# A fifth staging buffer for the rows of weights, and five list tiles a half for the batched heads, in a one-core decoder block

## The chip, the core and the metric

The kernel runs on one core of a Trainium2 chip. The metric is the device time of one execution in microseconds (us); three runs of the kernel before are at hand, and their median is what a changed kernel is compared with. The engines are named as in the profile: PE is the matrix engine and PEld its weight loads, DVE the vector engine, ACT the scalar engine, POOL the engine that issues the gathers, SP the one that issues most plain transfers.

## The reference

The kernel computes one decoder block over 1024 tokens of width 1024 in float32: a first part with gated linear attention and a spatial gate beside it, and then an expert mixer, whose lists of experts are what half of the change is about. Cut to what matters:

```
proj = h @ w_in                       # 1024 x 7184, then attention, gates, w_out
q  = (h2 @ w_q).reshape(T, 8 heads, 2, 128)
s1 = q[..., 0, :] @ keys1.T ; s2 = q[..., 1, :] @ keys2.T
v1, i1 = top_k(s1, 16) ; v2, i2 = top_k(s2, 16)
top_s, pos = top_k(v1[:, None] + v2[None, :], 16)    # per token and head
g = softmax(top_s)                                   # 16 weights
y = sum over heads and the 16 experts: g * gelu(expert_down[e] . h2) * expert_up[e]
```

With the scales of the inputs the softmax is steep: most of the 16 weights of a head are zero in float32. The kernel counts weights of at least 1.18e-38. Worked out from the reference's inputs, 65 heads of the first half of the tokens and 51 of the second still have an eighth weight that large; the kernel calls them rare. All their weights that large are 634 rows in the first half and 475 in the second.

## The kernel before

The tokens are worked off in two halves of 512. Each half streams its weights in rows of 128x512 float32 (256 KB): 14 groups of 8 for the projection, 32 for the output projection, 40 for the queries, so 184 for a half. Such a row goes through three stages. SP fetches it into one of `WT` staging buffers `wt` (line 1373, pool `wstage`, line 1055). ACT makes its rounded part `wh` (L1377) and DVE the rest `wl` (L1379), into one of `WS` = 4 pairs of buffers; a staging buffer is free again when `wl` has been made. PE then multiplies: 12 matrix products of 512 columns for a row, 6 in the output projection (L182, L183, L185, or L188 to L190 for the first and last rows of a group). `weights_ahead` keeps four rows (LOOK + 1) issued ahead of the one that is used.

The expert mixer works on list tiles of 128 experts. POOL gathers 1 MB for a tile (128 rows of `tab` with 8 KB each, `uv`, L526), or 512 KB twice (`uvu`, `uvv`) where the tile goes into two 4 KB buffers; PE brings the tokens' rows to the entries (`hps`, L579 and L580), DVE makes the dot products (L581), ACT the Gelu (L584), and PE adds the weighted rows up (L626 and L627 while the first part is still running, L607 afterwards). There are three kinds of tiles. Ordinary lists: 9 tiles (`NT`) for each block of 128 tokens. Direct tiles, the best expert of each head, one for each head of a block (`Wd`, L535 to L540; those of the first four blocks are made by `direct_rows`, L753 to L776, which only POOL, DVE and ACT work on). And the lists of the rare heads, batched for a half: `NTR` tiles, which read the table `thq`/`tlq` with 50 columns. Their room is `t * 128` rows for `t` tiles; `peer_rest` compares it with the counts and works everything off again in a slow loop if any list does not fit.

`peer_stream` writes the order of all tiles in one list `todo`: the rare tiles of the first half first, then the lists of blocks 0 to 3, then 12 direct tiles of later blocks, after which it waits until the first part is over (`HOLD`). This is called stage 1 here; in it `wh` and `wl`, attention and list tiles share the engines. The rest, from the gather of the 19th direct tile on, is stage 2. Which buffers a tile gets follows from its place k in `todo`: `RING[k % 6]` in stage 1, `RING9[k % 9]` in stage 2, where 0 is the pool of stage 1 (three buffers), 1 the 4 KB buffers and 2 the pool that opens with stage 2.

The program is recorded by Tile with a list scheduler, which orders the instructions of every engine by times that it expects, so a number at the top of the file can move instructions everywhere. Each engine then works in its written order, and so do POOL's gathers.

```
NTR = (6, 6)
WS = 4
WT = 4
RING = (1, 0, 1, 0, 2, 0)
RING9 = (2, 0, 1, 2, 0, 2, 1, 0, 2)
        seg(NBLK, range(PH, PH + NTR[0]))
        seg(NBLK + 1, range(PH, PH + NTR[1]))
        caps = [NT * P] * NBLK + [t * P for t in NTR] + [P] * NG
        wst_p = pa.enter_context(tc.tile_pool(name="wstage", bufs=WT))
```

Of the kernel before, what the change touches and what calls it, by code (L numbers as in the profile page):

```python
# [40 lines left out]
ROW0 = (0, 16, 24, 32, 40, 44, 48, 52, 56)  # L41
NC_ = 64
NT = 9
NTR = (6, 6)
EB = 2
WS = 4
WT = 4
RD = 0.62
UVC = 4
RING = (1, 0, 1, 0, 2, 0)  # L50
# [31 lines left out]
def block_kernel(ctx: ExitStack, tc: tile.TileContext, x, xT, cT, w_ada, b_ada, b_adaT, n1T, w_inp, w_alr,  # L82
# [697 lines left out]
    def peer_stream():  # L780
# [3 lines left out]
        def seg(b, js, open_=True, close=True):  # L784
            if open_:
                opens.add((b, js[0]))
            if js[0] < PH:
                runs.add((b, js[0]))
            todo.extend((b, j) for j in js)
            if close:  # L790
                closes.add((b, js[-1]))

        rows = range(PH, last + 1)
        seg(NBLK, range(PH, PH + NTR[0]))
        for b in range(BH):
# [8 lines left out]
        seg(BH + 1, range(PH, last))  # L804
        seg(NBLK + 1, range(PH, PH + NTR[1]))
        seg(BH + 2, range(PH, last - 1), close=False)
# [138 lines left out]
    def peer_rest(pl, pg_):  # L945
# [5 lines left out]
        morei = pc.tile([1, 1], I32, name="morei")  # L951
        caps = [NT * P] * NBLK + [t * P for t in NTR] + [P] * NG
        for i, c in enumerate(caps):
# [100 lines left out]
    with ExitStack() as pa:  # L1054
        wst_p = pa.enter_context(tc.tile_pool(name="wstage", bufs=WT))
        wsp = pa.enter_context(tc.tile_pool(name="wsplit", bufs=WS))
# [831 lines left out]
```

## Time and profile before

| what | value |
| --- | --- |
| three runs | 1444.07, 1448.06, 1449.47 us; median 1448.06 |
| the profiled execution | 1445.78 us, of which the profile's span is 1444.0 |
| instructions | 19662 |
| mean granted PE clock | 0.974 of full speed |
| matrix products of a row of weights, one line's group (L182) | 648, 397 ns each as recorded |
| gathers of 1 MB for list tiles | 73, 8.2 us from issue to landing in the median |

The profile's page lists busy time by engine, the chain of work that ended last, and the groups of equal instructions. Matrix products overlap, and a recorded duration is longer than the distance from one start to the next; that distance is read from the chain of waits or the timeline. A row of the timeline is: start, duration, engine, line, operation, tile written <- tiles read, count, and in brackets how long the engine had been idle before it and what ended that. A row of the waits is: who waited <- for whom: us in total, times, the longest.

### The profile page before, as it was taken

Reading aid. Unit: us, or ns where it says so; the run is one execution under the profiler, and the core shown is the slowest. Engines: PE = TensorE matmul, PEld = TensorE weight load, DVE = VectorE, ACT = ScalarE, POOL = GpSimd, SP = SyncE. Lnnn points to the kernel's source line nnn. Section 1 sums busy time; section 2 is a strip of 40 time slices with the busy share of each in tenths; the row PEclk is TensorE's granted clock in tenths of the full one; section 3 lists DMA queues with packets and bytes.
Section 4 is the critical chain, followed back from the end, with each engine's and each line's share of the span. In section 5 each row is a group of like instructions: output and inputs, shape, how many; then the busy total and the mean of one; then the engine's idle time right before and its main releaser. Section 6 shows DMA issues by size and latency. Waiting matters only on the chain.

```text
span 1444.0 us, 19662 instructions
## 1 busy us (share of the span) xinstructions
PE 1352.7 (94%) x6018; PEld 1041.6 (72%) x6018; DVE 1094.8 (76%) x3109; ACT 728.8 (50%) x1602; POOL 287.2 (20%) x276
## 2 busy tenths in 40 slices
PE   8999999999998999979989999899987999789996
PEld 6678777888887888767877878787766886445553
DVE  7885686433578589888889787778788877899775
ACT  4463333332455456456435677456545555546542
POOL 0100011000000111341542143211021114553331
PEclk9999999999999999999999999999999999999999
DMA  9743553322377675675777698886777658998984
GB/s 332 274 166 117 190 163 129 95 95 66 114 243 255 216 244 184 242 250 199 246 265 262 223 347 308 305 287 229 254 277 275 228 194 350 330 372 329 418 308 173
DMA packets 120980, 345.00 MB, mean 239 GB/s; under 512 B 15049, under 2 KB 24521, under 8 KB 108962
## 3 DMA queue, kind: packets, MB, share of 16 engines
q0 software_dynamic: 32208, 165.95, 31.5%
q1 hardware_dynamic: 71600, 133.43, 27.7%
q10 hardware_dynamic: 17058, 44.29, 8.5%
q8 instruction: 48, 0.79, 0.2%
q14 instruction: 66, 0.54, 0.1%
HBM read 319.40 MB, written 24.23 MB: 238 GB/s over the span
## 4 chain that ended last, share of the span: by engine, by line
PE 37%; DVE 9%; DMA 9%; issue 7%; ACT 4%; POOL 2%; SPq 0%; ACTq 0%; DVEq 0%; POOLq 0%
PE acc L607 6%; PE mm L182 5%; PE mm L183 5%; PE mm L185 5%; PE mm L188 2%; PE mm L189 2%; PE mm L190 2%; DMA uv<-in_tab_dram,ix 2%; PE aux L1781 2%; DMA uv<-in_tab_dram,dix 1%; DMA uvd<-in_down_dram,dix 1%; PE hps L579 1%; PE hps L580 1%; DVE uv L581 1%; DVE wl L1379 1%
## 5 line engine op out<-in xcount | busy, mean ns | idle before, releaser
L1377 ACT ACTIVATE wh<-wt 128x512 fp32r<-128x512 f32 x360 | 223.0, 628 | 333.8 <-PE mm L183 113.6
L1379 DVE TENSOR_TENSOR wl<-wt,wh 128x512 fp32r<-128x512 f32 x360 | 242.2, 683 | 140.9 <-ACT wh L1377 78.6
L182 PE MATMUL mm<-wh,hTh 128*128 128x512 f32 x648 | 256.9, 397 | 5.6 <-ACT wh L1377 5.6
L183 PE MATMUL mm<-wh,hTl 128*128 128x512 f32 x648 | 254.8, 394 | 0.0
L185 PE MATMUL mm<-wl,hTh 128*128 128x512 f32 x648 | 200.2, 396 | 0.0
L182 PEld LDWEIGHTS mm<-wh,hTh 128*128 128x128 f32 x648 | 122.3, 189 | 35.7 <-ACT wh L1377 7.7
L183 PEld LDWEIGHTS mm<-wh,hTl 128*128 128x128 f32 x648 | 122.1, 189 | 25.8 <-issue 0.7
L185 PEld LDWEIGHTS mm<-wl,hTh 128*128 128x128 f32 x648 | 121.1, 188 | 26.8 <-issue 0.7
L526 POOL DMA_INDIRECT uv<-in_tab_dram,ix x73 | 81.9, 1122 | 268.0 <-ACT ix L558 163.0
L182 PE MATMUL mm<-hTh,wh 128*128 128x512 f32 x240 | 96.5, 402 | 0.0
L183 PE MATMUL mm<-hTl,wh 128*128 128x512 f32 x240 | 96.2, 401 | 0.0
L188 PE MATMUL mm<-wh,hTh 128*128 128x512 f32 x216 | 86.8, 411 | 2.7 <-DVE sg L1605 1.0
L581 DVE SCALAR_TENSOR_TENSOR uv<-uv,hps 128x512 f32<-128x512 f32 x110 | 73.7, 680 | 17.4 <-PE hps L580 8.7
L189 PE MATMUL mm<-wl,hTh 128*128 128x512 f32 x216 | 85.5, 397 | 0.0
L190 PE MATMUL mm<-wh,hTl 128*128 128x512 f32 x216 | 85.4, 395 | 0.0
L188 PE MATMUL mm<-hTh,wh 128*128 128x256 f32 (+1 forms) x208 | 72.1, 350 | 12.6 <-DVE q L1509 7.8
L189 PE MATMUL mm<-hTl,wh 128*128 128x256 f32 (+1 forms) x208 | 70.4, 340 | 3.3 <-DVE hTl L174 3.3
L753 POOL DMA_INDIRECT uvd<-in_down_dram,dix x32 | 36.9, 1154 | 174.2 <-DVE cidx L354 38.2
L185 PE MATMUL mm<-hTh,wl 128*128 128x512 f32 x240 | 71.0, 397 | 0.0
L190 PE MATMUL mm<-hTh,wl 128*128 128x256 f32 (+1 forms) x208 | 69.1, 339 | 0.3 <-DVE wl L1379 0.3
L619 DVE SCALAR_TENSOR_TENSOR vl<-uv,r,vh 128x512 fp32r<-128x512 f32 x82 | 59.9, 745 | 11.9 <-ACT vh L618 5.7
L579 PE MATMUL hps<-hh,E 128*128 128x512 f32 x132 | 61.3, 465 | 6.1 <-DVE uv L581 2.8
(971 smaller groups left out, 2936.4 us busy)
## 6 DMA issues: line engine op xcount, KB each, us to landing
wt<-in_w_inp_dram SPq DMA_DIRECT2D x224, 256.0 KB, 3.5
wt<-in_w_qp_dram SPq DMA_DIRECT2D x80, 256.0 KB, 4.9
wada<-in_w_ada_dram SPq DMA_DIRECT2D x32, 512.0 KB, 5.3
wt<-in_w_outp_dram SPq DMA_DIRECT2D x64, 256.0 KB, 3.8
wada<-in_w_ada_dram SPq DMA_DIRECT2D x32, 256.0 KB, 5.7
s_d<-so ACTq DMA_DIRECT2D x28, 256.0 KB, 2.6
xr<-in_x_dram ACTq DMA_DIRECT2D x8, 512.0 KB, 4.6
x_d<-x ACTq DMA_DIRECT2D x8, 512.0 KB, 4.2
```

The source lines that it names most:

```text
L182: nc.tensor.matmul(ps, lh, rh, start=False, stop=False)
L183: nc.tensor.matmul(ps, *((lh, rl) if feat else (ll, rh)), start=False, stop=False)
L185: nc.tensor.matmul(ps, *((ll, rh) if feat else (lh, rl)), start=False, stop=False)
L188: nc.tensor.matmul(ps, lh, rh, start=first, stop=False)
L189: nc.tensor.matmul(ps, lh, rl, start=False, stop=False)
L190: return nc.tensor.matmul(ps, ll, rh, start=False, stop=last).ins
L526: nc.gpsimd.indirect_dma_start(out=dst[:], out_offset=None, in_=src, in_offset=off)
L579: nc.tensor.matmul(hps, Ej, hh[:, sl], start=True, stop=False)
L581: nc.vector.scalar_tensor_tensor(uv[0][:, sl], uv[0][:, sl], 1.0, hps, op0=OP.mult, op1=OP.mult, accum_out=r[:, 2 + n:3 + n])
L607: ins = nc.tensor.matmul(acc[:, sl], W, v[:, sl], start=first, stop=last).ins
L1377: nc.scalar.activation(wh, wt, AF.Identity)
L1379: nc.vector.tensor_tensor(wl, wt, wh.bitcast(F32), op=OP.subtract)
```

## The change

Two numbers at the top of the file:

```
-NTR = (6, 6)
+NTR = (5, 5)
 EB = 2
 WS = 4
-WT = 4
+WT = 5
```

`WT = 5` adds a staging buffer of 2 KB in each partition. `NTR = (5, 5)` takes the sixth list tile of the rare heads out of each half: 2 of 1 MB gathers (the two 512 KB gathers of a tile count as one), and on PE 2 times 2 products of L549/L550, 8 of L579/L580 in all, 4 of L626/L627 in the first half and 4 of L607 in the second, with their dots and Gelus on DVE and ACT. The room for rare rows is then 640 in each half. Every later tile moves up one place in `todo` (two places behind the second half's rare tiles), and so takes another turn of `RING` or `RING9`.

On SP, at the start of the weights of the first half (L1089 is the hand-ordered first group, `wada` are rows of the modulation's weights):

```order
 L1089 DMA wada<-in_w_ada_dram 128x2x256 x8
-L1089 DMA wt<-in_w_inp_dram 128x512
-L1108 DMA wada<-in_w_ada_dram 128x1024
-L1089 DMA wt<-in_w_inp_dram 128x512
+L1089 DMA wt<-in_w_inp_dram 128x512 x2
 L1089 DMA wal<-in_w_al_dram 16x512
 L1089 DMA balt<-in_b_alT_dram 128x4
 L1089 DMA keyst<-in_keysT_dram 128x256
 L1089 DMA sgub<-in_sgu_bT_dram 128x8
-L1373 DMA wt<-in_w_inp_dram 128x512 x4
+L1108 DMA wada<-in_w_ada_dram 128x1024
+L1373 DMA wt<-in_w_inp_dram 128x512 x5
```

Five rows of weights now go out in one go where four did, and a `wada` row that stood between two of them moved behind the first group.

On ACT, in the second half while `direct_rows` runs (`rdr` is a direct tile's Gelu, `dt`, `eGi`, `egl` the exponentials that the attention's products wait for, `wh` the rounded weights):

```order
-L770 ACTIVATE yd<-uvd,rdr 128x1024
 L1567 ACTIVATE egl_5818<-G_5482 128x4x2
 L1522 ACTIVATE eGi<-G_5458 128x512
-L1523 ACTIVATE dt<-dt 128x512 x2
+L1523 ACTIVATE dt<-dt 128x512
+L767 ACT_TABLE_LOAD
+L767 ACTIVATE rdr<-rdr 128x1
+L1523 ACT_TABLE_LOAD
+L1523 ACTIVATE dt<-dt 128x512
 L1377 ACTIVATE wh<-wt 128x512 x3
 L767 ACT_TABLE_LOAD
```

A Gelu now stands between the two `dt`, with a load of the function table on each side of it, and ahead of three conversions of weights.

On POOL, where stage 2 begins, the first gather into the new pool is the row that waits for many transfers (DMAHW) and engines at once. Before:

```order
L526 DMA uvv<-in_up_dram,dix_2_137 128x1024 [waits DMASW3_49,DVE_49]
L526 DMA uv<-in_tab_dram,dix_2_137 128x2048 [waits DMAHW2_49,DMAHW3_49,DMAHW1_49,DMAHW5_49,DMAHW0_49,DMAHW6_49,DMASW4_49,DMAHW7_49,PE_49,Activation_49]
L526 DMA uv<-in_tab_dram,dix_2_137 128x2048 [waits DMASW5_49,PE_49]
L526 DMA uv<-in_tab_dram,dix_2_137 128x2048 [waits DMASW7_49,DMASW6_49,PE_49]
L526 DMA uv<-in_tab_dram,dix_3_138 128x2048 [waits DVE_49]
```

and of the change:

```order
L526 DMA uvu<-in_down_dram,dix_2_137 128x1024 [waits DMASW0_49,DVE_49]
L526 DMA uv<-in_tab_dram,dix_2_137 128x2048 [waits DMAHW3_49,DMAHW2_49,DMAHW4_49,DMAHW1_49,DMAHW5_49,DMAHW0_49,DMAHW6_49,DMASW1_49,DMAHW7_49,PE_49,Activation_49]
L526 DMA uv<-in_tab_dram,dix_2_137 128x2048 [waits DMASW2_49]
L526 DMA uv<-in_tab_dram,dix_2_137 128x2048 [waits DMASW3_49,PE_49]
L526 DMA uvv<-in_up_dram,dix_2_137 128x1024 [waits DMASW4_49,DVE_49]
```

Before, the gather into the new pool is followed by two that wait for PE to be through with a buffer of the old pool; now the next one waits for no engine, and only the one behind it does.

## The prediction

> **What bounds the kernel now.** First the page: busy time by engine, the chain of work that ended last, and the transfers.
>
> ```profile
> PE 1352.7 (94%) x6018; PEld 1041.6 (72%) x6018; DVE 1094.8 (76%) x3109; ACT 728.8 (50%) x1602; POOL 287.2 (20%) x276
> ...
> PE 37%; DVE 9%; DMA 9%; issue 7%; ACT 4%; POOL 2%; SPq 0%; ACTq 0%; DVEq 0%; POOLq 0%
> ...
> DMA packets 120980, 345.00 MB, mean 239 GB/s; under 512 B 15049, under 2 KB 24521, under 8 KB 108962
> ```
>
> PE is busy for 94% of the span by the record. Its idle time is thus 91 us of 1444. So the kernel is bound by PE, and a change pays in two ways: it takes products away, or it closes one of PE's gaps. Second, stretches by windows (start and end, length, busy us of PE, PEld, DVE, ACT, POOL, the granted PE clock, the DMA engines' busy share, GB/s), where the change touches something:
>
> ```profile
> 300.00:400.00 100.00, 100.00 (x482) 84.00 (x481) 44.07 (x87) 35.69 (x59) 0.00 (x0) 1.00 0.30 97
> ...
> 640.00:650.00 10.00, 2.48 (x11) 1.71 (x10) 8.14 (x24) 3.12 (x7) 3.06 (x3) 0.77 1.03 405
> ...
> 770.00:800.00 30.00, 28.96 (x130) 23.79 (x129) 29.68 (x68) 18.14 (x38) 8.85 (x7) 1.00 0.73 251
> ...
> 1055.00:1060.00 5.00, 2.95 (x13) 2.07 (x12) 3.38 (x8) 0.51 (x1) 1.00 (x1) 1.00 1.04 413
> ...
> 1250.00:1255.00 5.00, 3.71 (x9) 1.80 (x10) 4.39 (x36) 2.66 (x8) 1.15 (x2) 1.00 0.80 306
> 1255.00:1260.00 5.00, 1.71 (x4) 0.40 (x3) 4.84 (x29) 3.49 (x5) 4.08 (x4) 0.98 0.94 318
> ...
> 1320.00:1356.00 36.00, 35.35 (x126) 20.72 (x125) 30.81 (x135) 19.65 (x71) 18.02 (x19) 1.00 0.99 397
> ```
>
> From 300 to 400 us, in the first half of the tokens, where no list tiles run, PE has no gap at all and the transfers are at 0.30; nothing is to be won there. Where the first rare tiles run (770 to 800 us), PE and DVE are both full. Where the second ones run (1320 to 1356), PE is full and the transfers nearly so. In between lie gaps: at 640, at 1055, at 1250, each time with the transfers at 0.8 to 1.04 of what they can do.
>
> **The list tiles.** The chain around 1335 us, in order of time (start, us, what), and the rare tiles' own group:
>
> ```profile
> 1336.86 1.72 PE acc L607 x4
> ...
> 1338.71 0.33 PE hps L579
> 1339.03 0.23 PE hps L580
> ...
> 1339.50 0.23 PE hps L580
> ...
> 1339.73 1.72 PE acc L607 x4
> ...
> L549 PE MATMUL tps<-thq,E x6: 587/587/587, 1332.3 to 1346.6; 128*128 128x50 f32 x6
> ```
>
> The six tiles of the second half's rare heads lie between 1332.3 and 1346.6, on PE and on the chain without a break, one every 2.87 us (1336.86 to 1339.73). One fewer is **-2.9 us**. If the transfers set the pace there instead, 1 MB at 397 GB/s is 2.6 us, so the bounds are -2.6 and -2.9, and I take PE's.
>
> A tile of the first half costs PE 8 products of 512 columns: four `hps`, and four of L626/L627. At 0.23 us from start to start (the L580 above) that is 1.84, and the two narrow products of L549/L550 add about 0.1: **-1.9 us**. DVE loses two dots of 0.68 and two splits of 0.745 (groups below), about 2.9 us with what stands between them, so DVE, full there as well, doesn't hold the gain back. Bounds: 0, if another wait takes its place, and -2.9, DVE's share.
>
> ```profile
> L581 DVE SCALAR_TENSOR_TENSOR uv<-uv,hps 128x512 f32<-128x512 f32 x110 | 73.7, 680 | 17.4 <-PE hps L580 8.7
> ...
> L619 DVE SCALAR_TENSOR_TENSOR vl<-uv,r,vh 128x512 fp32r<-128x512 f32 x82 | 59.9, 745 | 11.9 <-ACT vh L618 5.7
> ```
>
> **The fifth staging buffer.** It lets SP fetch a row of weights when the `wl` five rows back is made, not four. It can pay only where PE waits for a conversion that waits for a transfer. Waits of ACT and PE over the whole program, PE's two rows at 1060 us, and the `wl` that free the buffers there:
>
> ```profile
> ACT wh L1377 <- DMA wt<-in_w_inp_dram: 42.8, 20, 5.2
> ...
> ACT wh L1377 <- DMA wt<-in_w_outp_dram: 23.9, 15, 5.5
> ...
> PE mm L182 <- ACT wh L1377: 5.6, 3, 3.1
> ...
> 1060.17 0.50 PE L182 MATMUL mm<-wh,hTh 128*128 128x512 f32 x1 [2.22 <-ACT wh L1377]
> ...
> 1064.61 0.79 PE L182 MATMUL mm<-wh,hTh 128*128 128x512 f32 x1 [3.09 <-ACT wh L1377]
> ...
> 1052.06 11.79 DMA wt<-in_w_outp_dram
> ...
> 1065.41 0.43 PE mm L183
> ...
> 1050.75 1.28 DVE L1379 TENSOR_TENSOR wl<-wt,wh 128x512 fp32r<-128x512 f32 x2
> ```
>
> ACT waits 67 us for rows of weights in these two groups, but PE only 5.6 us for ACT, and 5.3 of them are the two rows at 1060. So nearly all of ACT's waiting is already hidden behind split rows in stock. The chain there runs through one transfer of 11.79 us, in a stretch where the engines move 413 GB/s. The second stall ends when that row lands. With a fifth buffer it goes out one `wl` earlier, and two `wl` make 1.28 us, so 0.64; and one row less is queued ahead of it, 0.262 MB at 413 GB/s = 0.63. Together -1.3 us; closing the first stall brings PE only sooner to the second. With the third of PE's waits (0.3) that is **-1.6 us**. The bounds: 0, and all of it, 5.6 us, plus the slower pace behind the stall, where seven products stand 0.43 apart and not 0.23, 1.4 us: -7.0. The value near the low end follows the full transfer engines at 1055.
>
> On this the Trainium skill ("DMA: Bandwidth & Descriptors", section "Issuing engines are not separate DMA queues") says that transfers from every issuing engine end up on the same 16 DMA engines and interleave. The 413 GB/s at a share of 1.04 agree: a transfer that starts earlier takes the place of another one there. By this rule the buffer brings nothing in a full stretch, which is rival 1.
>
> **The turn of the buffers at the start of stage 2.** Three rows of POOL and one of PE:
>
> ```profile
> 1243.72 0.94 POOL L526 DMA_INDIRECT uv<-in_tab_dram,dix  x1 [1.55 <-PE aux L1781]
> ...
> 1246.67 0.94 POOL L526 DMA_INDIRECT uv<-in_tab_dram,dix  x1 [2.00 <-PE acc L607]
> ...
> 1253.55 0.94 POOL L526 DMA_INDIRECT uv<-in_tab_dram,dix  x1 [5.94 <-PE acc L607]
> ...
> 1260.90 3.75 PE L607 MATMUL acc<-uv,Wd 128*128 128x512 f32 x4 [4.20 <-issue]
> ```
>
> The first gather into the new pool goes out at 1243.72. The next two wait 2.00 and 5.94 us for PE to release a buffer of the old pool, and POOL's whole queue stands behind them, while PE runs dry for 4.20 us at 1256.7. In the changed order the second gather goes into the new pool too and waits for no engine. What this can win is the transfer time that lay idle: 5 us at 0.80 and 5 us at 0.94 leave 1.3 us. **-1.3 us**; bounds 0 (the transfers are full right behind) and -4.2, PE's whole gap.
>
> **Everything else that moves.** The other moves on the engines I cost at 0 in the middle, since each Gelu and conversion is still there once; the shown place on ACT adds two table loads of 1.28 us to an engine that is half idle. Where that cover is gone is rival 2.
>
> The sum: -2.9 - 1.9 - 1.6 - 1.3 = **-7.7 us**. The profiled execution of 1445.78 us, span and what lies around it, becomes 1438.1. It lies 2.3 us below the median of the three runs, 1448.06, to which the same -7.7 gives **1440.4 us**. A measurement of this kernel can tell about 0.5%, 7.2 us, from no change, so the forecast is barely outside that.
>
> **Rival 1: the fifth row only displaces gathers.** For it: the full stretches at 640 and 1055. In 900 to 1130 us the chain runs through long landings of gathers:
>
> ```profile
> 988.54 7.67 DMA uv<-in_tab_dram,ix
> ...
> 1029.57 8.93 DMA uv<-in_tab_dram,ix
> ...
> 1111.12 7.61 DMA uv<-in_tab_dram,ix
> ```
>
> If each of the three lands one row later (0.63), the change gives back 1.9, staging wins nothing, and the turn of the buffers nothing either: -2.9 - 1.9 + 1.9 = -2.9, 1445.2 us. Against it: over the span the transfers run at 239 GB/s, so most extra rows find room.
>
> **Rival 2, slower: a Gelu ahead of the conversions on ACT.** Its place is 620 to 700 us, where `direct_rows` shares ACT with the attention. A Gelu there waits for DVE's dot, the dot for a gather, and ACT works in order, so everything behind it stands too.
>
> ```profile
> ACT rdr L767 <- DVE uvd L765: 23.7, 10, 6.2
> ...
> PEld mm L188 <- ACT rdr L767: 8.2, 1, 8.2
> ...
> 650.26 0.76 PE L188 MATMUL mm<-hTh,wh 128*128 128x512 f32 x1 [7.78 <-DVE q L1509]
> ...
> 626.72 1.14 ACT L1523 ACTIVATE dt<-dt 128x512 f32<-128x512 f32 x2
> ...
> 627.98 1.22 DVE L765 SCALAR_TENSOR_TENSOR uvd<-uvd,h2d 128x1024 f32<-128x1024 f32 x1
> ```
>
> Before, such waits came to 23.7 us on ACT and reached PE once, for 8.2 us. In the changed order a Gelu stands ahead of a `dt` that was made before 627.9, while the dot it needs began at 627.98: with 1.2 us for the dot and two loads of 1.28 the `dt` and three conversions come nearly 5 us later. It decides when the Gelu's wait outlasts the split rows in stock, four at 12 times 0.23 us, 11 us. One more stall of 8.2 us eats the gain (1448.6), two make it slower: -7.7 + 16.4 = +8.7, 1456.8 us. Against it: in that same gap PE's product was released by DVE, so ACT was not last even there, and one place in ACT's order need not make two stalls.
>
> **Rival 3: the order falls well.** The gaps close to their bounds: -2.9 - 1.9 - 7.0 - 4.2 = -16.0, 1432.1 us. The gap at 650 us, behind which DVE stood, could add to this:
>
> ```profile
> 641.86 0.49 DVE L205 MAX8 qtv<-qsc 128x8 f32<-128x128 f32 x2 [3.34 <-DMA qsc<-s_d,qix]
> ```
>
> DVE waits 3.34 us there for the rare heads' scores, and its new order puts two more dots ahead of that wait. But those dots need gathers that land late themselves, at 405 GB/s, so I count nothing for it.
>
> **Rival 4: five tiles don't hold the rows.** Then the slow loop runs: 8 blocks times 128 gathers of 1 MB, 2.6 us each at 397 GB/s, 2.7 ms more, beyond 4100 us. Worked out from the inputs, the first half needs 634 of 640 rows and the second 475. The rows nearest to the limit are four with weights 1.4 to 1.6 times too small, and with all of them the count would be 638, so this takes weights that are wrong by more than a factor of two.
>
> **How the numbers follow.** The forecast, between 1436 and 1445, has 0.45, of which three quarters lie below 1440.8, the bound of 0.5%. Rival 3 has 0.14, rival 1 0.24, rival 2 0.16, rival 4 0.01. Faster by over 0.5%: 0.14 + 0.34 = 0.48. Slower: 0.16 + 0.01 = 0.17. Within: 0.35. The range reaches from 1430, just below rival 3, to 1455, which takes in one stall of rival 2 and most of the second; it leaves out about 0.15.
>
> **What would show it.** The rare tiles at 2.87 us in the tail, five of them, the first term. PE's waits for `wh` well below 5.6 us in total and the two stalls in the second output projection shorter by 1.3 together: the third; unchanged, rival 1, with gathers that land later than 8.2 us in the median. The second gather of stage 2 right behind the first, and PE's gap of 4.2 us shorter: the fourth. A weight load that waits 8 us for a Gelu more than once: rival 2. The prediction is wrong if the first half changes by more than 2 us, or if gaps move about in the second half by more than the terms above: then the order set the result and the sum was beside it.

## The result, and the profile after

The change takes **1429.42 us** in the median of four runs (1427.28 to 1432.73), the kernel before 1448.7 (1444.07 to 1449.47): the ratio is 0.9871, with a 95% interval of 0.9847 to 0.9895. On a second occasion, beside the parts of the change, it was 0.9902 (0.9864 to 0.9940). By the ratios the change gains 18.7 us in one measurement and 14.2 in the other (by the medians 19.3 and 15.6), where 7.7 were forecast. The profiled execution took 1432.73 us, its span is 1431.0 and its mean clock 0.978; that is 13.0 us of span less than before.

The page of the change, first its engines, its chain and its transfers:

```profile
PE 1346.4 (94%) x5998; PEld 1037.3 (72%) x5998; DVE 1087.9 (76%) x3088; ACT 724.6 (51%) x1590; POOL 288.0 (20%) x271
...
PE 33%; DVE 13%; DMA 11%; issue 6%; ACT 4%; POOL 1%; ACTq 0%; DVEq 0%; POOLq 0%; SPq 0%
...
DMA packets 120548, 343.96 MB, mean 240 GB/s; under 512 B 15001, under 2 KB 24473, under 8 KB 108402
```

PE has 20 products less and bounds the kernel as before. The rare tiles of the tail in the timeline (start, duration, engine, line, operation) and the group they form (shortest, median and longest duration in ns, first and last start), then ACT's waits for rows of weights, and PE's for DVE's `q` and for `wh`:

```profile
1323.67 0.59 PE L549 MATMUL tps<-thq,E 128*128 128x50 f32 x1
1326.55 0.59 PE L549 MATMUL tps<-thq,E 128*128 128x50 f32 x1
...
1335.23 0.59 PE L549 MATMUL tps<-thq,E 128*128 128x50 f32 x1
```

```profile
L549 PE MATMUL tps<-thq,E x5: 587/587/588, 1323.7 to 1335.2; 128*128 128x50 f32 x5
```

```profile
ACT wh L1377 <- DMA wt<-in_w_outp_dram: 14.6, 12, 2.5
...
ACT wh L1377 <- DMA wt<-in_w_inp_dram: 11.3, 6, 2.5
...
ACT wh L1377 <- DMA wt<-in_w_qp_dram: 7.3, 5, 2.6
```

```profile
PE mm L188 <- DVE q L1509: 7.2, 1, 7.2
...
PE mm L188 <- ACT wh L1377: 1.2, 1, 1.2
...
PE mm L182 <- ACT wh L1377: 0.3, 1, 0.3
```

Five tiles, 2.9 us apart. ACT's wait for rows of the projection fell from 42.8 to 11.3 us and for those of the output projection from 23.9 to 14.6. PE's wait for `wh` fell from 5.6 us, all at L182, to 1.5, of which 0.3 are at L182 and 1.2 at L188. PE's long wait at 650 us, for DVE's `q`, is there once as before (7.8 then, 7.2 now). Windows at the places shown of before (start and end, length, busy us of PE, PEld, DVE, ACT, POOL, granted PE clock, share of the DMA engines, GB/s; the last is the rare tiles' stretch, taken 10 us earlier; the tiles start 8.6 us earlier):

```profile
640.00:650.00 10.00, 2.79 (x12) 2.09 (x11) 6.89 (x20) 4.17 (x8) 4.87 (x5) 0.83 1.03 403
770.00:800.00 30.00, 29.62 (x133) 24.10 (x132) 28.23 (x66) 18.09 (x38) 7.06 (x7) 1.00 0.74 256
1055.00:1060.00 5.00, 4.70 (x21) 3.54 (x20) 5.00 (x11) 2.60 (x5) 0.95 (x1) 1.00 0.94 345
1310.00:1346.00 36.00, 35.58 (x121) 20.14 (x121) 30.42 (x130) 19.78 (x70) 15.93 (x17) 1.00 1.00 405
```

At 640 us PE stands as before, with the transfers full; at 1055 it is now busy (4.70 of 5 us, 2.95 before).

**Where the time went.** For each product of PE I take the distance from the end of the product before to its own end. What exceeds the usual distance of its kind (the first quartile in the trace of before) is called stall; it holds idle time and the slower products behind it. The sum of the usual distances is called work. The span is cut by program places, the starts of `wl` (L1379, 360 in all, counted from zero) and of the direct tiles; the times are those of the trace of before. Two numbers in a cell are two profiled executions, of which the second comes from a run below.

| stage (us in the trace of before) | before | change |
| --- | --- | --- |
| A: to the 96th `wl` (0 to 365) | 18.1, 20.2 | 19.7, 19.7 |
| B: turn of the halves, 96th to 184th (to 583) | 16.9, 20.6 | 14.4, 18.2 |
| C: to the 264th (to 887) | 31.0, 30.0 | 35.2, 35.0 |
| D: to the 296th (to 1022) | 15.9, 16.9 | 15.4, 15.6 |
| E: second output projection and most queries, to the 344th (to 1162) | 31.3, 27.9 | 19.1, 17.6 |
| F: to the 19th direct tile (to 1261) | 6.4, 4.3 | 8.7, 7.3 |
| G: to the end | 27.5, 29.1 | 26.8, 27.9 |
| all stalls | 147.1, 148.9 | 139.3, 141.3 |
| work | 1283.8, 1283.8 | 1278.7, 1278.5 |

Of about 13 us, 5.2 are work, close to the 4.8 that the two tiles should bring. The other 7.7 are stalls: 11.2 us less in E and 2.4 less in B, 4.6 more in C and 2.6 more in F, the rest in A, D and G. Two executions of one kernel agree within about 2 us in most stages, in B, D and E within 4, and in the sum of all stalls within 6 (`o4b5` below), so a difference of that size between two single traces shows little.

### The profile page after: what moved, and what is told of

Its sections match the earlier page's. It is cut to its first block, busy times and chain, and to the rows that moved or that the text cites. A ratio compares the mean times of both kernels' runs of the same rounds, so it can differ in the third digit from the quotient of the medians.

```text
span 1431.0 us, 19574 instructions
## 1 busy us (share of the span) xinstructions
PE 1346.4 (94%) x5998; PEld 1037.3 (72%) x5998; DVE 1087.9 (76%) x3088; ACT 724.6 (51%) x1590; POOL 288.0 (20%) x271
## 3 DMA queue, kind: packets, MB, share of 16 engines
q1 hardware_dynamic: 71600, 133.43, 27.9%
## 4 chain that ended last, share of the span: by engine, by line
PE 33%; DVE 13%; DMA 11%; issue 6%; ACT 4%; POOL 1%; ACTq 0%; DVEq 0%; POOLq 0%; SPq 0%
PE acc L607 5%; PE mm L182 4%; PE mm L183 4%; PE mm L185 4%; DMA uvd<-in_down_dram,dix 3%; DMA uv<-in_tab_dram,dix 2%; PE mm L188 2%; PE mm L189 2%; PE mm L190 2%; DMA uv<-in_tab_dram,ix 2%; PE hps L579 1%; PE aux L1781 1%; DVE wl L1379 1%; PE hps L580 1%; DMA fin<-y_d 1%
## 5 line engine op out<-in xcount | busy, mean ns | idle before, releaser
L1379 DVE TENSOR_TENSOR wl<-wt,wh 128x512 fp32r<-128x512 f32 x360 | 241.5, 684 | 127.0 <-PE mm L185 61.4
L182 PE MATMUL mm<-wh,hTh 128*128 128x512 f32 x648 | 255.9, 395 | 0.3 <-ACT wh L1377 0.3
L182 PEld LDWEIGHTS mm<-wh,hTh 128*128 128x128 f32 x648 | 122.0, 188 | 29.2 <-issue 2.8
L182 PE MATMUL mm<-hTh,wh 128*128 128x512 f32 x240 | 95.7, 399 | 0.0
L188 PE MATMUL mm<-wh,hTh 128*128 128x512 f32 x216 | 86.4, 409 | 8.0 <-ACT sg L1613 3.3
L581 DVE SCALAR_TENSOR_TENSOR uv<-uv,hps 128x512 f32<-128x512 f32 x112 | 74.7, 680 | 24.2 <-DMA uv<-in_tab_dram,ix 17.8
L188 PE MATMUL mm<-hTh,wh 128*128 128x256 f32 (+1 forms) x208 | 71.5, 346 | 11.3 <-DVE q L1509 7.2
L607 PE MATMUL acc<-uv,W 128*128 128x512 f32 x132 | 63.5, 603 | 2.2 <-ACT W L596 1.8
L579 PE MATMUL hps<-hh,E 128*128 128x512 f32 x128 | 58.7, 458 | 6.1 <-ACT ts__9523 L552 2.0
```

The source lines that it names most:

```text
L182: nc.tensor.matmul(ps, lh, rh, start=False, stop=False)
L188: nc.tensor.matmul(ps, lh, rh, start=first, stop=False)
L579: nc.tensor.matmul(hps, Ej, hh[:, sl], start=True, stop=False)
L581: nc.vector.scalar_tensor_tensor(uv[0][:, sl], uv[0][:, sl], 1.0, hps, op0=OP.mult, op1=OP.mult, accum_out=r[:, 2 + n:3 + n])
L607: ins = nc.tensor.matmul(acc[:, sl], W, v[:, sl], start=first, stop=last).ins
L1379: nc.vector.tensor_tensor(wl, wt, wh.bitcast(F32), op=OP.subtract)
```

## The experiments

Three theories stood at the start. *Staging*: the fifth buffer closes stalls. *Turn*: the shifted places in `RING` and `RING9` make the gain. *Order*: any number rearranges the queues, and this one fell well. All ratios are against the kernel before on the same chip, with 95% intervals; a gain in us is worked out from the ratio.

**The two numbers apart.** `wt5` has `WT = 5` alone, `ntr55` has `NTR = (5, 5)` alone.

```
-WT = 4          # wt5
+WT = 5
-NTR = (6, 6)    # ntr55
+NTR = (5, 5)
```

> The kernel before with WT = 5 alone; six rare tiles a half stay. Staging theory (the fifth buffer closes PE's stalls between 1040 and 1165 us, where the trace of the change gains 10 us on the trace of before): about 14 us less than before, near 1434.5 us, PE's waits for wh below 1 us, and the 128x512 rows of weights used between 1060 and 1165 us 8 to 15 us ahead of before. Turn theory (the places of the list tiles in RING and RING9, which this kernel leaves as they were, make the gain): within 3 us of before. Order theory (any number that rearranges the queues moves the time by several us either way, and the change fell well): anywhere from -10 to +10 us, with the gain or loss spread over other places than 1060 to 1165 us.

> The kernel before with NTR = (5, 5) alone; four staging buffers stay. Staging theory: about 5 us less than before (2.9 in the tail and at most 2 in the first half), near 1443.5 us, and the two PE stalls for wh at 1060 us, 5.3 us together, are still there. Turn theory: nearly all of the gain, 15 to 19 us less, near 1431 us. Order theory: 5 us less give or take 8, with the gaps of the second half in other places than in either trace.

`wt5` 0.989 (0.9849 to 0.9932), `ntr55` 0.9883 (0.9847 to 0.9920). Each alone gives nearly the whole gain, so the two don't add. Stage E has 21.7 us of stalls in `wt5`, and 17.1 in `ntr55`, with four buffers. This spoke against the first two theories in their simple form: the staging theory expected 5 us from `ntr55` and the turn theory nothing from `wt5`.

**The turn of the buffers alone.** `after_turn` gives every list tile of the change the place in the ring that it had before; `before_turn` does the opposite to the kernel before.

```
-[RING[k % len(RING)] ...
+[RING[(k + (k >= NTR[0]) + (k > rare2)) % len(RING)] ...
-[RING9[k % len(RING9)]]
+[RING9[(k + (k >= NTR[0]) + (k > rare2)) % len(RING9)]]
```

(`rare2` is the place of the last rare tile; in `before_turn` the two signs are minus.)

> The changed kernel, but every list tile behind the rare ones takes the turn of RING or RING9 that it had before (one place on behind the first half's rare tiles, two behind the second's). Staging theory: within 3 us of the change, near 1430 us; if the shifted turn was worth something where stage 2 begins, 1 to 4 us more. Turn theory: 10 us or more above the change, 1440 and more. Order theory: a difference of several us either way that no one place explains.

> The kernel before, but every list tile behind the rare ones takes the turn of RING or RING9 that the change gives it; six rare tiles a half and four staging buffers stay. Staging theory: within 3 us of before; at most 1 to 4 us less where stage 2 begins, if the second gather into the new pool no longer waits for PE. Turn theory: 10 to 15 us less than before. Order theory: a difference of several us either way.

`after_turn` 0.9839 (0.9799 to 0.9880), so taking the shift back costs nothing; `before_turn` 0.9956 (0.9928 to 0.9985), a gain of 6 us in the kernel before, where the turn theory expected 10 to 15. The turn theory falls as the source of the change's gain; what the shift brought in `before_turn` can be its own order too, since these two kernels were scheduled anew.

**How far a trace can be trusted, and one tile at a time.** `before2` and `after2` are the two kernels unchanged; `ntr56_wt5` and `ntr65_wt5` are the change with a sixth tile put back in one half.

> The kernel before once more, with a profile of another execution. All theories: the same stalls of PE at the same places as in the first trace. If its stall time by stage differs by more than 3 us from the first trace in some stage, differences of that size between two kernels' traces show nothing.

> The change once more, beside the kernel before on the same chip as the parts of it. All theories: near 0.987 of before. It is the base for the two kernels below, which differ from it by one rare tile each; if the parts add up (0.989 and 0.988), it is 0.977.

> The change, but with six rare tiles in the second half. Its order is nearly that of the change (132 rows of difference on PE). First term of the prediction: 2.9 us slower than the change, the six tiles again 2.87 us apart in the tail and all that stands ahead of them unchanged within 1 us. Order theory: not 2.9 us but anything from -3 to +8.

> The change, but with six rare tiles in the first half. Second term of the prediction: 1.9 us slower than the change. Staging theory: the stalls between 1040 and 1165 us stay closed as in the change, since the fifth buffer closes them. Order theory: several us either way, since its order differs from the change in 3132 rows on PE; the stall time of single stages moves by 3 us or more.

`before2` took 1447.38 us; its stages and those of `after2` are the second numbers in the table above. `ntr56_wt5` has 0.9911 (0.9877 to 0.9946), beside 0.9902 for the change: the medians are 3.8 us apart, not more than their scatter, but in the profile the stretch from the first to the last rare tile has 13.8 us of work in place of 11.1, so 2.7 for the tile. `ntr65_wt5` has 0.9928 (0.9900 to 0.9955) and 2.2 us more work than the change. The terms of the tiles are thus right in size as work on PE, 2.7 and 2.2; the medians don't resolve them.

**The order held.** To part the buffer from the order that it brings about, each engine's instructions were tied to a written order, those of another build of the same program. Only issue order is added, no wait.

```
+for a, b in zip(names, names[1:]):      # one engine's instructions, in the written order
+    tc.add_manual_dep(traced[b], a, DependencyInfo(DependencyClass.NoSync, ...))
```

`o4b5` has five buffers in the order of before. `o5b4` has four in the order of `wt5`, `oab4` five tiles and four buffers in the order of the change; in these two SP is free, because an order planned five rows ahead cannot be kept with four, and in their traces some 10 of SP's 466 DMAs stand elsewhere.

> The kernel before with five staging buffers, but every engine's instructions held in the order of the kernel before, word for word (issue order alone, no waits are added). Staging theory: the stalls between the 296th and 344th row of weights, 31 us before, fall by 8 us or more, and the time by 9 to 15 us. Order theory (WT = 5 alone gained because it made another order): within 4 us of before, and the stalls of that stretch stay at 27 us or more. The prediction's third term: 1.6 us less.

> The kernel before with its four staging buffers and six rare tiles, but PE, DVE, ACT and POOL held in the order that WT = 5 alone gives them (SP is left free, since its order of five rows ahead cannot be kept with four buffers). Staging theory: no gain, within 3 us of before. Order theory: the gain of WT = 5 alone, 9 to 15 us less than before. Both in part: in between.

> Five rare tiles a half and four staging buffers, with PE, DVE, ACT and POOL held in the order of the change (SP is left free). Staging theory: the stalls between 1040 and 1165 us come back, 8 us or more above the change, near 0.996 of before. Order theory: within 4 us of the change, 0.987 to 0.992 of before.

`o4b5` **0.9883** (0.9848 to 0.9918), `o5b4` **1.0091** (1.0055 to 1.0127), `oab4` **1.0031** (1.0009 to 1.0053). PE, DVE, ACT and POOL stand alike in each pair, and in `o4b5` SP too, so the fifth buffer is worth 17 us in the order of before. In the change's own order it is worth 1.3 to 1.6%, together with SP's moved DMAs and with an order that was planned for five buffers; without it the change would be no faster than before. The order theory falls for the buffer. It holds for something else: `oab4` and `ntr55` have the same work and buffers, and lie 1.5% apart.

> The change with four rare tiles in the second half in place of five: 512 rows of room where 475 are needed. First term of the prediction: 2.9 us less than the change, four tiles 2.87 us apart in the tail. Order theory: from -6 to +6 us beside the change, though its order should differ little, since these tiles stand late in the list.

`ntr54_wt5` 0.9898 (0.9864 to 0.9932): the fourth tile less shows in the profile (8.3 us of work between the rare tiles, 2.8 less than the change), not in the medians.

**Where the fifth buffer pays.** The staging theory looked for the gain in E, but in `o4b5` the stalls of E hardly change. Those of B do:

| stage | before | `o4b5` | `o4b5_xlate` | `x_early` | `oab4` | change |
| --- | --- | --- | --- | --- | --- | --- |
| B | 16.9, 20.6 | 10.0, 10.6 | 17.0 | 14.7 | 20.4 | 14.4, 18.2 |
| C | 31.0, 30.0 | 32.7, 32.8 | 28.8 | 35.0 | 40.2 | 35.2, 35.0 |
| E | 31.3, 27.9 | 27.7, 28.1 | 27.5 | 25.1 | 24.2 | 19.1, 17.6 |
| F | 6.4, 4.3 | 4.4, 4.1 | 10.6 | 4.6 | 7.2 | 8.7, 7.3 |
| all stages | 147.1, 148.9 | 135.5, 141.4 | 148.1 | 142.9 | 155.0 | 139.3, 141.3 |

The timeline of before at the turn of the halves, first SP (`SPq` is its queue; the last number is how many DMAs), then ACT, then PE:

```profile
489.23 2.58 SPq L1373 DMA_DIRECT2D wt<-in_w_qp_dram  x3
491.86 1.85 SPq L1196 DMA_DIRECT2D xb<-in_x_dram  x4
493.77 3.81 SPq L1203 DMA_DIRECT2D xt<-in_xT_dram  x4
...
497.40 1.06 ACT L1197 ACTIVATE xb<-xb 128x1024 f32<-128x1024 f32 x1 [2.13 <-DMA xb<-in_x_dram]
...
504.87 1.06 ACT L1197 ACTIVATE xb<-xb 128x1024 f32<-128x1024 f32 x1 [1.43 <-DMA xb<-in_x_dram]
...
506.44 2.04 ACT L1733 ACTIVATE qt<-mm 128x512 f32<-128x512 f32 x4
...
507.07 1.22 PE L1781 MATMUL aux<-keyst,qt 128*128 128x128 f32 x4 [3.73 <-ACT qt L1733]
...
508.94 0.63 PE L190 MATMUL mm<-hTh,wl 128*128 128x512 f32 x1
509.37 0.63 PE L182 MATMUL mm<-hTh,wh 128*128 128x512 f32 x1
```

Here the second half's `x` is loaded (L1196 and L1203, eight DMAs of 512 KB). SP works in order, and the loads stand behind three rows of weights that wait for a staging buffer. ACT works in order too: its four squares of `x` (L1197) wait for the loads, and `qt` stands behind them. PE waits 3.73 us for `qt`, in the second execution 6.4, and then runs its products 0.43 us apart (508.94 to 509.37). The same places in `o4b5`:

```profile
486.42 1.99 SPq L1373 DMA_DIRECT2D wt<-in_w_qp_dram  x2
488.46 1.85 SPq L1196 DMA_DIRECT2D xb<-in_x_dram  x4
...
492.41 1.06 ACT L1197 ACTIVATE xb<-xb 128x1024 f32<-128x1024 f32 x1
...
499.61 1.06 ACT L1197 ACTIVATE xb<-xb 128x1024 f32<-128x1024 f32 x1 [1.42 <-DMA xb<-in_x_dram]
...
501.19 2.04 ACT L1733 ACTIVATE qt<-mm 128x512 f32<-128x512 f32 x4
...
501.81 0.71 PE L1781 MATMUL aux<-keyst,qt 128*128 128x128 f32 x4 [1.30 <-ACT qt L1733]
...
502.83 0.40 PE L190 MATMUL mm<-hTh,wl 128*128 128x512 f32 x1
503.06 0.40 PE L182 MATMUL mm<-hTh,wh 128*128 128x512 f32 x1
```

Only two rows of weights wait ahead of the loads; the third went out at 478.24 us instead of 489.23, while the transfers were half idle (a share of 0.51 from 470 to 480 us, 0.34 from 480 to 490). PE waits 1.30 us, and its products are at once 0.23 apart (502.83 to 503.06). Windows of the same 30 us, first of before, with its slow stretch in a row of its own, then of `o4b5`:

```profile
490.00:520.00 30.00, 26.27 (x115) 21.69 (x114) 16.87 (x84) 16.33 (x29) 5.68 (x5) 0.89 0.84 308
505.50:512.00 6.50, 4.93 (x14) 4.07 (x15) 2.77 (x6) 5.61 (x10) 1.05 (x1) 0.50 1.05 390
```

```profile
490.00:520.00 30.00, 28.70 (x143) 24.01 (x142) 21.69 (x96) 18.78 (x34) 4.73 (x5) 1.00 0.93 343
```

115 products against 143, the granted clock 0.89 against 1.00, 308 GB/s against 343; from 505.5 to 512 us the clock of before stands at 0.50. Of the 8.5 us that B loses in `o4b5`, 6.1 lie at this place: the four rows of weights around it have 6.5 and 8.9 us of stalls in the two traces of before, 1.7 and 1.5 in those of `o4b5`.

Two kernels tried this path, two more whether it is still open in the change; all are held in the order named, and only SP's `x` loads move (where they move forward, the tie to the last row of weights, at L1195 and L1202, is taken out). In `x_early` they stand three rows of weights earlier, with four buffers; in `o4b5_xlate` one row later, with five.

```
 L1373 DMA wt<-in_w_qp_dram      # x_early, SP's order
+L1196 DMA xb<-in_x_dram x4
+L1203 DMA xt<-in_xT_dram x4
 L1373 DMA wt<-in_w_qp_dram x3
-L1196 DMA xb<-in_x_dram x4
-L1203 DMA xt<-in_xT_dram x4
```

> The kernel before with four staging buffers, all engines held in its own order, but on SP the eight loads of the second half's x (L1196, L1203) stand three rows of weights earlier. Queue theory (the fifth buffer gains around 507 us of the trace, since a row of weights that waits for a staging buffer holds the x loads behind it in SP's queue, ACT waits in its order for x ahead of qt, and PE waits for qt and is then slow): the wait of 3.7 to 6.4 us of PE for qt there falls to 1.3 or less, the stall time between the 96th and the 184th row of weights from 17 to 21 us to about 10, and the time falls by 6 to 10 us with four buffers. Stock theory (the fifth buffer gains by rows in stock everywhere): within 3 us of before, or slower, since the rows of weights behind the x loads come later.

> Five staging buffers in the order of the kernel before, but on SP the eight x loads stand one row of weights later, so that with five buffers they wait for the same wl as with four. Queue theory: half or more of the gain of the fifth buffer is lost; 0.988 of before becomes 0.992 to 0.997, and PE's wait for qt near 505 us is back at 3 us or more. Stock theory: 0.988 stays within 0.003.

> The change, held in its own order, with the eight x loads three rows of weights earlier on SP. Queue theory: PE's two waits for qt in that stretch (3.7 to 5.3 us together, and the slow products behind them) go, 3 to 6 us less than the change, near 0.984 of before. Stock theory: no gain, 0.987 to 0.990.

> The change with the buffers' turn of before (0.984 of before by itself), held in its own order, with the eight x loads three rows of weights earlier on SP. Queue theory: 3 to 6 us less again, near 0.980, the fastest of these kernels. Stock theory: 0.984 within its interval.

`o4b5_xlate` 0.9948 (0.9924 to 0.9971): about half of the gain is gone (`o4b5` has 0.9883, and 0.9906 when it was run again), PE's wait for `qt` is 5.8 us, the stalls of the four rows around it are back at 8.6 us and stage B at 17.0. But F is 6 us worse in its trace as well, which I can't explain by the moved loads. `x_early` 0.9994 (0.9968 to 1.0021): no gain. Its ACT and PE at the same place:

```profile
500.74 0.63 ACT L1377 ACTIVATE wh<-wt 128x512 fp32r<-128x512 f32 x1 [4.79 <-DMA wt<-in_w_qp_dram]
...
507.10 0.71 PE L1781 MATMUL aux<-keyst,qt 128*128 128x128 f32 x4 [3.11 <-ACT qt L1733]
```

Now `x` is in time and a row of weights late behind it; ACT waits 4.79 us for that row, and `qt` comes no sooner. In this one trace the clock stayed at 1.00 behind the wait of 3.11 us, and the four rows have only 3.4 us of stalls, but the medians of twelve runs show nothing of it. So my queue theory was half right. What the fifth buffer gives is not the earlier place of `x` in the queue alone, but one row more that is fetched in the quiet time ahead of 4 MB of `x`; with four buffers `x_early` only handed the wait from one load to the other.

`after_x` 0.9874 (0.9837 to 0.9910) and `after_turn_x` 0.9836 (0.9794 to 0.9878): no gain that the medians show, although stage B falls to 11.2 us in the trace of `after_x`. What stays of the queue theory there is too small for these intervals, or is taken back elsewhere.

> The kernel before with five staging buffers in its own order, once more, on another occasion: 0.988 of before again (0.985 to 0.992), and in a second profile the stall time between the 96th and the 184th row of weights again 7 us or more below the 17 to 21 us of before. If the time comes out above 0.994, the first measurement was a chance, and the fifth buffer alone is worth no more than the kernel with the x loads one row later shows.

> The change with four rare tiles in the second half and the buffers' turn of before: its order is that of the kernel with the turn of before (0.984) but for the last rare tile. One tile less in the tail, 2.9 us, 0.2%: near 0.982, the fastest of the kernels tried.

`o4b5_again` 0.9906 (0.9870 to 0.9942), stage B 10.6: the buffer's worth repeats, 13.6 us here and 17 there. `ntr54_turn` 0.9844 (0.9805 to 0.9882), 1425.77 us, is the fastest median of all the kernels, but on another chip; by the ratio it is no faster than `after_turn` (0.9839) and `after_turn_x` (0.9836), and its tile less shows again in the profile only.

## Why the prediction was wrong

**The direction and two terms were right.** The tail's tile: -2.9 forecast, 2.7 measured between the rare tiles. The first half's tile: -1.9 forecast, 2.2 by the work of `ntr65_wt5`. Together 4.8 against 5.2 us of work.

**The third term failed.** The sentence was: the fifth buffer "can pay only where PE waits for a conversion that waits for a transfer", and "nearly all of ACT's waiting is already hidden behind split rows in stock". From this came 1.6 us, at 1060 us, with 7.0 as the far end. In the order of before the buffer brought 17 and 13.6 us, by the traces 9.6 of stalls (148.0 to 138.5), of which 8.5 lie in stage B (18.8 to 10.3). By these traces 6.1 of them stand where PE's row reads "3.73 <-ACT qt", and I took that for a wait of another kind. But ACT stands in order: `qt` waited behind squares that waited for loads, and these stood on SP behind rows that waited for a buffer. I followed ACT's waits to PE by one tile's name and not by ACT's queue. The order of SP's DMAs shows the `x` loads between rows of weights; the prediction did not use it there.

At its own place, 1060 us of before, `o4b5` shows this on PE (`ts` is a list tile's rows of the table, which ACT copies out of PE's result):

```profile
1052.04 0.50 PE L182 MATMUL mm<-wh,hTh 128*128 128x512 f32 x1 [0.95 <-ACT wh L1377]
...
1056.56 0.80 PE L579 MATMUL hps<-hh,E 128*128 128x512 f32 x1 [3.33 <-ACT ts__10211 L552]
```

PE waits only 0.95 us for `wh`, where it was 5.3, but then 3.33 for `ts`: a stall was handed on. Stage E falls by 1.7 us, from 29.6 to 27.9. That this is near the 1.6 of the forecast is luck: the way was another, and two executions differ by up to 3.4 us there. The 11 us that E lost in the change need the change's order and tiles: with that order and four buffers (`oab4`) it stands at 24.2, so about 6 of the 11 come with the buffer and 5 with order and tile, a split that rests on one trace, in which SP's order differs too. By which waits the buffer closes E in that order is not shown.

**The price of a stall was too low.** I counted the slow products only as an upper bound at one place. Behind the wait of 3.73 us at 507 us the products of the next 5 us lose another 2.4, in `o4b5` behind 1.30 us only 0.3: 4.5 us for a wait that got 2.4 shorter. On this the Trainium skill ("TensorE: Matmul & The Clock Gate", section "Part 1: The HAM clock gate (the "warmup" mystery)") says that PE falls to half its clock after an idle window of about 3.4 us, and needs as long a busy one to come back. The two traces agree: 0.43 us from product to product behind 3.73 us, with the granted clock at 0.50, and 0.23 behind 1.30, with the clock at 1.00.

**The fourth term came and was lost.** POOL and PE of the change where stage 2 begins:

```profile
1237.37 0.94 POOL L526 DMA_INDIRECT uv<-in_tab_dram,dix  x1 [5.30 <-PE aux L1781]
1238.62 0.93 POOL L526 DMA_INDIRECT uv<-in_tab_dram,dix  x1 [0.30 <-issue]
1239.85 0.94 POOL L526 DMA_INDIRECT uv<-in_tab_dram,dix  x1 [0.30 <-issue]
...
1251.66 1.98 PE L607 MATMUL acc<-uv,Wd 128*128 128x512 f32 x4 [2.70 <-ACT Wd L540]
1260.09 0.59 PE L314 MATMUL aux<-cnt,ltri 128*128 128x4 f32 x2 [4.72 <-DVE cnt L308]
```

The second and third gather follow the first without a wait for PE, as forecast, and the waits of 2.00 and 5.94 us are gone; the first itself now waits 5.30 us for PE, where it was 1.55. But PE's gap is still there: 4.72 us, now for DVE's count. A product that needs the count (L314) stands ahead of direct tiles that it followed before; whether PE would run sooner without it was not tried. F and G together are no shorter than before, and `after_turn`, which takes the shift back, is not slower.

**The rivals.** Rival 2 did not happen: PE's wait of 8 us at 650 is there once, and DVE ends it as before. Rival 1, that the fifth row only displaces gathers, is refuted by `o4b5`. Rival 3 had the sum about right (-16.0, 1432.1 us) by luck, by the wrong path: it closed the gap at stage 2, which stayed, and gave the buffer 7.0. "Everything else" at 0 was wrong too: stage C became 4.6 us longer. By my own last sign, gaps moved about by more than the terms, so the sum alone could not have been trusted.

**Still open:** why the change gains more by its ratios (18.7 and 14.2 us) than by its two pairs of profiles (13.0 and 12.9), and `o4b5` more (17 and 13.6) than by the stalls of its traces (9.6), so that a part of the buffer's worth has no place; whether `qt` ahead of the squares in ACT's order would bring the same with four buffers, which was not tried; what moved stage F in `o4b5_xlate`; and why the planner's order for five tiles and four buffers (`ntr55`) is as good as a fifth buffer.

## What to carry to other kernels

Before a buffer is priced at the waits that name its tile, follow the queues behind it: whatever stands on the issuing engine behind a load that waits for a buffer waits too, and the engine in front of the bound one hands that on under another name. A change of buffers and the order that a scheduler makes of it can be parted by holding the order; without that, each of two parts seemed to bring the whole gain. Price a stall of the matrix engine with the slow products behind it, which came to 2.2 us in the mean behind gaps over 3.3 us here.

## What the runs showed of the hardware

In the twenty traces PE has 85 gaps longer than 3.3 us. Behind every one the granted clock stands at 0.5, and the products of the next 5 us lose 1.7 to 2.7 us more, 2.2 in the mean. Behind gaps of 2 to 3.3 us there is such a loss (over 0.9 us) in 57 of 95; the clock stands at 0.5 behind 55 of these 57 and behind one of the other 38. No other value than 0.5 and 1.0 is recorded, and 234 of the 254 stretches at 0.5 last 3.4, 6.8 or 10.2 us. The section of the Trainium skill named above calls its window free-running, and that fits the middle group, where gaps of like length are punished or not: in the trace of before the one of 3.09 us at 1064 us loses 2.1, the one of 3.18 at 1251 us 0.3.
